# A gated SSD layer on one core: turnings in one step, TensorE's order tied to each chunk, time-step products in score banks, and fewer stores

## The chip, the cores and the metric

The kernel runs on one core of a Trainium2 chip. The metric is the device time of one launch in microseconds, as the median of several runs. The engines are TensorE (PE, with its weight loads shown as PEld), VectorE (DVE), ScalarE (ACT), GpSimd (POOL) and SyncE (SP), which issues most of the DMAs.

## The reference

A small diffusion backbone of two layers over 1024 latent and 256 context tokens, 1024 wide. Layer 0 is gated windowed attention. Layer 1 is a gated state-space mixer (SSD) that scans in both directions. Each layer is: norm, modulation, mixer, gated residual add. The part that the change touches is layer 1's front and chunk pass:

```python
z, xbc, dt_raw = jnp.split(h @ w_in, [SSD_WIDTH, SSD_WIDTH + SSD_CONV_DIM], axis=-1)
xbc = jax.nn.silu(centred_depthwise_conv(xbc, conv_w, conv_b))     # 5 taps
xs, bm, cm = jnp.split(xbc, ...)
dt = jax.nn.softplus(dt_raw... + dt_bias_dir)
...
a_cs = jnp.cumsum(da, axis=2)                                      # per chunk of 128
states = jnp.einsum('bcsgn,bcsgr,bcsgrp->bcgrpn', bm, decay_to_end, xdt)
h = exp(a_last) * h + states                                       # scan over chunks
cb = jnp.einsum('bcqgn,bcsgn->bcqsg', cm, bm)
y_diag = jnp.einsum('bcqsg,bcqsgr,bcsgrp->bcqgrp', cb, lmat, xdt)
y_off = jnp.einsum('bcqgn,bcgrpn,bcqgr->bcqgrp', cm, h_prev, jnp.exp(a_cs))
```

There are 8 groups of 4 heads of 64, a state of 128, 8 latent chunks of 128 tokens and 2 context chunks. All is float32.

## The kernel before, in words

Large products are split: each operand is a high part in a fast form and a low part, and three products (high by high, low by high, high by low) add up in one bank. `weights` makes the parts of a weight tile: ScalarE casts the high part (L1034), VectorE subtracts for the low part (L1038). There are two buffers of each.

Layer 1 goes through the groups. While group g's eight chunks run (`slot`, once a chunk), the projections of group g+1 (`front`) fill TensorE between a chunk's steps. `front` is a generator: each `next` issues one product and yields its cost, and `run` in the main loop takes as many as the chunk's share. Its products are:

- L1085, a context tile, 24 products of 256 columns into a bank called psD, of which there is one buffer,
- L1095, the two latent tiles of 512 columns, into pj (two buffers),
- L1129, the z gate, 192 products of 256 columns.

Each finished tile goes through side steps kept in the queue `post`, which lets one go after so much TensorE work: a first tap on ScalarE (L1007), four taps on VectorE (L1011), tanh on ScalarE (L1018), product on VectorE (L1019), and then `natural`: the tile is turned by TensorE (L1058) into the bank that its raw product came from, and ScalarE copies it out (L1061), into bn or xn.

A chunk (`slot`) consists of the opening products pcb (L1247) and po (L1249 from the forward state hf, L1250 from the backward state hb), the state product L1256, four head products L1281 against the masked decay tile M, and the turning of the chunk before (L1312, copied by ScalarE's L1313). M is made from rows loaded from DRAM: `load_rows` (L1221), an offset on POOL (L1226), a merge on VectorE (L1230), four exponentials on ScalarE (L1236), the product with pcb (L1251). VectorE also makes L1260, L1266, L1292 and L1293 of each chunk, and the z gate's product L1140.

`states` is the chain that carries the states from chunk to chunk: product L1198 into psD, decay on POOL, addition on VectorE (L1210) or a copy on ScalarE (L1202). Each L1198 needs the psD buffer back from the step ahead.

Ahead of group 0 stands the time step. `dt_raw` adds the bias on ScalarE (L923) to 3 products per slice of a narrow weight (`proj`, L246 to L248). The `dt_chain` steps (VectorE L974 to L987, among them the reciprocal L980) make softplus, decays and running sums, and store the sums and the totals to DRAM, from where the rows of M and the totals (eal) are loaded. `dt_tail` spaces these steps by DTPACE. Layer 0 ends with a norm whose sum is L363 and whose spread is L380.

The order of the instructions on each engine is set by a scheduler at build time from the program's order and the tiles' dependencies. `issue_after(x)` holds what is issued in its block behind instruction x. Each engine then executes its list in that order.

## Time and profile before

| | before |
|---|---|
| median of 3 runs | 1810.02 us (1809.37 to 1811.35) |
| profiled execution | 1807.02 us |
| its span | 1805.3 us |
| mean granted clock | 0.993 |
| first pcb (L1247) of groups 0, 1, 2, 3 at | 849.29, 954.77, 1060.54, 1166.32 us |

The profiled execution is 1.7 us longer than its span and 3.0 us below the median. The times of layer 1 lie between about 735 us and the end. The pcb starts show the length of a group, some 105.7 us, of which nearly all is TensorE work.

### The profile page before, as it was taken

The page shows a single profiled execution, that of the slowest core. Times are in us where ns is not written, and L with a number is a line of the kernel's source. Part 1 is how long each engine was busy: PE and PEld are TensorE (multiplying, and loading weights), DVE is VectorE, ACT ScalarE, POOL GpSimd, SP SyncE. Part 2 cuts the span into 40 slices and gives each one's busy share as a digit, 9 for nine tenths or more (in the row PEclk, how much of TensorE's full clock was granted, in tenths as well). Part 3 has the DMA queues.
Part 4 walks back from the last instruction along what each step waited for, and adds up shares of the span by engine and source line. Part 5 has one row for each costly group of instructions (what it writes and reads, how often), then busy time and mean ns, then how long its engine had stood idle before and what let it go on. Part 6 is the DMA issues. An engine that isn't in the chain of part 4 may idle for free.

```text
span 1805.3 us, 28983 instructions
## 1 busy us (share of the span) xinstructions
PE 1739.6 (96%) x10319; PEld 1494.7 (83%) x10319; DVE 1181.8 (65%) x2115; ACT 867.1 (48%) x1906; POOL 799.0 (44%) x1068
## 2 busy tenths in 40 slices
PE   6899999999999999999999999999999999999997
PEld 2697788888888887778888898988889898888887
DVE  4634436778877885684776858577684867766734
ACT  3612237777777774452443525344353534544522
POOL 2331127555575545103454544645454464554411
PEclk9999999999999999999999999999999999999999
DMA  9558856444455436222222323222332322656533
GB/s 334 226 144 268 283 177 149 106 100 111 111 153 130 120 102 221 73 53 73 71 77 82 92 62 98 79 71 79 81 93 62 100 73 76 174 169 170 175 101 121
DMA packets 212495, 227.61 MB, mean 126 GB/s; under 512 B 16384, under 2 KB 149632, under 8 KB 212352
## 3 DMA queue, kind: packets, MB, share of 16 engines
q1 hardware_dynamic: 178288, 207.12, 38.0%
q0 software_dynamic: 34064, 18.65, 5.8%
q8 instruction: 81, 1.33, 0.3%
q14 instruction: 62, 0.51, 0.1%
HBM read 190.88 MB, written 35.13 MB: 125 GB/s over the span
## 4 chain that ended last, share of the span: by engine, by line
PE 81%; DVE 9%; ACT 4%; DMA 3%; issue 2%; SPq 1%; POOL 1%; DVEq 0%; ACTq 0%; POOLq 0%
PE pj L1095 17%; PE pj L1129 10%; PE pj L1527 7%; PE pj L246 6%; PE pj L247 6%; PE pj L248 6%; PE psD L1085 4%; PE psX L1281 3%; PE pt L684 3%; PE psD L1198 2%; PE pv L691 2%; PE pv L690 1%; PE S L659 1%; PE S L658 1%; PE psX L1249 1%
## 5 line engine op out<-in xcount | busy, mean ns | idle before, releaser
L246 PE MATMUL pj<-uH,wh 128*128 128x512 f32 (+1 forms) x712 | 257.4, 363 | 9.0 <-ACT uH L470 6.3
L247 PE MATMUL pj<-uL,wh 128*128 128x512 f32 (+1 forms) x712 | 243.3, 342 | 0.5 <-POOL uL L707 0.4
L248 PE MATMUL pj<-uH,wl 128*128 128x512 f32 (+1 forms) x712 | 242.4, 341 | 1.4 <-POOL wl L231 1.4
L1095 PE MATMUL pj<-uH,wl 128*128 128x512 f32 x512 | 172.7, 405 | 0.0
L1095 PE MATMUL pj<-uH,wh 128*128 128x512 f32 x512 | 171.4, 405 | 1.2 <-ACT bn L1061 0.7
L1095 PE MATMUL pj<-uL,wh 128*128 128x512 f32 x512 | 169.2, 402 | 0.0
L246 PEld LDWEIGHTS pj<-uH,wh 128*128 128x128 f32 x712 | 135.6, 191 | 36.2 <-ACT uH L470 7.7
L1129 PE MATMUL pj<-wh,uH 128*128 128x256 f32 x512 | 150.3, 294 | 9.1 <-ACT xn L1061 9.1
L1173 POOL TENSOR_TENSOR xw<-xn,dtdec 128x256 f32<-128x256 f32 x144 | 92.9, 650 | 141.6 <-PE psD L1198 107.1
L1129 PE MATMUL pj<-wh,uL 128*128 128x256 f32 x512 | 152.7, 298 | 0.0
L248 PEld LDWEIGHTS pj<-uH,wl 128*128 128x128 f32 x712 | 135.0, 190 | 18.6 <-POOL wl L231 2.3
L247 PEld LDWEIGHTS pj<-uL,wh 128*128 128x128 f32 x712 | 135.8, 191 | 16.0 <-issue 3.0
L1129 PE MATMUL pj<-wl,uH 128*128 128x256 f32 x512 | 146.7, 287 | 0.0
L689 DVE TENSOR_TENSOR pl<-pt,ph 128x512 fp32r<-128x512 f32 x168 | 114.1, 688 | 47.2 <-ACT ph L688 46.2
L231 POOL TENSOR_TENSOR wl<-wr,wh 128x512 fp32r<-128x512 f32 x76 | 100.2, 1322 | 86.1 <-ACT wh L229 85.2
L663 DVE CUSTOM_DVE_ANT_0 sm<-S,mask,nsink 128x640 f32<-128x640 f32 (+2 forms) x160 | 119.2, 773 | 19.8 <-PE S L659 12.6
L665 ACT ACTIVATE sm<-sm,nm 128x640 f32<-128x640 f32 (+2 forms) x160 | 118.6, 742 | 16.6 <-DVE nm L663 15.9
L688 ACT CAST ph<-pt 128x512 fp32r<-128x512 f32 x168 | 97.5, 586 | 56.0 <-PE pt L684 52.7
L229 ACT CAST wh<-wr 128x512 fp32r<-128x512 f32 (+1 forms) x116 | 74.7, 648 | 87.7 <-PE pj L247 63.5
L1095 PEld LDWEIGHTS pj<-uH,wl 128*128 128x128 f32 x512 | 95.3, 188 | 19.2
L1095 PEld LDWEIGHTS pj<-uL,wh 128*128 128x128 f32 x512 | 95.4, 188 | 18.7
L1129 PEld LDWEIGHTS pj<-wh,uH 128*128 128x128 f32 x512 | 98.7, 193 | 13.5 <-ACT xn L1061 12.1
(339 smaller groups left out, 4810.8 us busy)
## 6 DMA issues: line engine op xcount, KB each, us to landing
wr<-w_x SPq DMA_DIRECT2D x32, 512.0 KB, 4.6
M<-acs SPq DMA_DIRECT2D x64, 256.0 KB, 4.9
bw<-acs SPq DMA_DIRECT2D x64, 256.0 KB, 5.5
wr<-w_sk SPq DMA_DIRECT2D x24, 512.0 KB, 3.8
wr<-wg SPq DMA_DIRECT2D x40, 256.0 KB, 4.5
qs<-q POOLq DMA_DIRECT2D x40, 256.0 KB, 3.9
wada<-w_ada SPq DMA_DIRECT2D x16, 512.0 KB, 7.2
wr<-wq SPq DMA_DIRECT2D x32, 256.0 KB, 3.0
```

The source lines that it names most:

```text
L231: (eng or nc.vector).tensor_tensor(l, raw, h, op=ALU.subtract)
L246: self.nc.tensor.matmul(ps, lh, rh, start=first and i == 0, stop=False)
L247: self.nc.tensor.matmul(ps, lh, rl, start=False, stop=False)
L248: self.last_mm = self.nc.tensor.matmul(ps, ll, rh, start=False, stop=last and i == n - 1)
L663: nc.vector.tensor_tensor_reduce(out=sm[:, :W], in0=Sv, in1=self.mask[:, m0 : m0 + W], scale=-SCALE, scalar=self.nsink[:, 4 * j + r : 4 * ...
L665: nc.scalar.activation(sm[:, :W], sm[:, :W], AF.Exp, bias=nm[:, r : r + 1], scale=-1.0, accum_out=sums[:, r : r + 1])
L688: nc.scalar.copy(ph, ptf)
L689: nc.vector.tensor_sub(pl, ptf, ph)
L1095: nc.tensor.matmul(raw[:, 512 * i : 512 * i + 512], l[:, k, :], r[i][:, k, :], start=k + y == 0, stop=k == KT - 1 and y == 2)
L1129: nc.tensor.matmul(pj[:, c], l, r[:, k, :], start=c % 2 + q + k + y == 0, stop=c % 2 == 1 and q == 1 and k == 3 and y == 2)
L1173: nc.gpsimd.tensor_tensor(xw, X(st, c).rearrange("p (r h) -> p r h", r=R), self.dtdec[:, c, hd(d, g)].unsqueeze(2).broadcast_to([P, R, HP] ...
L1527: nc.tensor.matmul(banks[x], l[:, z, sl], r, start=k == 2 * qs[0] and y == 0, stop=k == 2 * qs[-1] + 1 and y == 2)
```

## The change

It has five parts.

1. `natural` issues all the turnings of a tile in one step, and then the copies. Before, a tile with two destinations was turned by halves, with a copy behind each half.
2. TensorE's order is tied per chunk: every piece that `run` takes from `front` or `ssd_out` is held behind the latest L1250 (`self.opened`), and pcb is held behind the latest such product (`self.pe`).
3. The time-step products move from the start of layer 1 into the end of layer 0, in score banks (tag S): those of the context tile ahead of the last norm, and those of the first latent tile in two halves, one behind the norm's sum and one behind its spread (`dt_first`).
4. The time-step chain: 1/(1+e) and two operations become a tanh on ScalarE and two fused operations; the rows of M are asked for directly behind the running sums' store, not at the end; the stores become 4 (from 8) and 2 (from 12), with EPOS for the changed column order; DTPACE goes from 1.0 to 1.6.
5. The first merge is held behind the last silu product (`silu_last`).

```diff
-DTPACE = 1.0
+DTPACE = 1.6
+EPOS = (0, 1, 5, 6, 3, 4, 8, 9, 2, 7)
...
-                for f in steps:
+                for f in steps[:1] + ([self.dt_first] if i == 1 else []) + steps[1:]:
                     f()
...
             self.dt_setup()
-            for i, lo in ((2, 256), (0, 0)):
-                n = TT[i][1] // 2
-                self.dt_raw(self.dts[:, lo : lo + n], self.proj(ps, self.wdt, i), n)
+            raw = self.proj(ps, self.wdt, 2, "S")
+
+            def dt_first():
+                self.dt_raw(self.dts[:, 256:384], raw, 128)
+                out = []
+                half = self.proj_g(out, ps, [self.wdt], self.uH, self.uL, 0, "S", parts=2)
+                with self.tc.issue_after(self.summed.ins):
+                    next(half)
+                with self.tc.issue_after(self.spread.ins):
+                    next(half, None)
+                self.dt_raw(self.dts[:, :256], out[0], 256)
...
         def decay():
-            for o in (0, 384):
-                for y in range(4):
-                    d, s = y // 2, (o // 384) * 512 + 256 * (y % 2)
-                    nc.sync.dma_start(self.acs_d[32 * d : 32 * d + 32, s : s + 256], w3[32 * y : 32 * y + 32, o : o + 256])
+            for d in range(2):
+                for o in range(2):
+                    dst = self.acs_d[32 * d : 32 * d + 32, 512 * o : 512 * o + 512].rearrange("r (h n) -> h r n", h=2)
+                    nc.sync.dma_start(dst, w3[64 * d : 64 * d + 64, 384 * o : 384 * o + 256])
...
+            for d in range(2):
+                nc.sync.dma_start(self.eal_d[0, 32 * d : 32 * d + 32].rearrange("r (h k) -> h r k", h=2), et[64 * d : 64 * d + 64])
...
+            lambda: act(wr, w1, AF.Tanh, scale=-0.5),
             lambda: act(w1, w1, AF.Exp),
...
-            lambda: v.reciprocal(w3, w2),
-            lambda: v.tensor_mul(w1, w1, w3),
-            lambda: v.tensor_add(w1, w1, ea),
+            lambda: v.scalar_tensor_tensor(w1, in0=wr, scalar=1.0, in1=w1, op0=ALU.add, op1=ALU.mult),
+            lambda: v.scalar_tensor_tensor(w1, in0=w1, scalar=0.5, in1=ea, op0=ALU.mult, op1=ALU.add),
...
             decay,
+            rows,
             total,
...
             lambda: act(ea, w3, AF.Exp),
-            rows,
...
-            def tr(lo, hi):
-                for x in range(lo, hi):
+
+            def tr():
+                for x in range(n):
                     nc.tensor.transpose(raw[:, x * P : (x + 1) * P], acc[:, x * P : (x + 1) * P], self.ident)
...
-            for d, lo, hi in dst:
-                steps.append(lambda lo=lo, hi=hi: tr(lo, hi))
-                steps.append(lambda d=d, lo=lo, hi=hi: ev(d, lo, hi))
-            return [(LATE, steps)]
+            return [(LATE, [tr] + [lambda d=d, lo=lo, hi=hi: ev(d, lo, hi) for d, lo, hi in dst])]
...
-            nc.tensor.matmul(pcb, st["bT"][:, cs], st["cT"][:, cs], start=True, stop=True)
+            with self.tc.issue_after(self.pe.ins):
+                nc.tensor.matmul(pcb, st["bT"][:, cs], st["cT"][:, cs], start=True, stop=True)
...
-            nc.tensor.matmul(po[:, 256:], st["cT"][:, cs], flat(st["hb"][c]), start=True, stop=True)
+            self.opened = nc.tensor.matmul(po[:, 256:], st["cT"][:, cs], flat(st["hb"][c]), start=True, stop=True)
...
-        merge(fw[0], bw.pop(0))
+        with self.tc.issue_after(self.silu_last.ins):
+            merge(fw[0], bw.pop(0))
...
                     while spent < until:
-                        cost = next(work, None)
-                        if cost is None:
-                            return
-                        spent += cost
-                        post.run(cost)
+                        with self.tc.issue_after(self.opened.ins):
+                            cost = next(work, None)
+                            if cost is None:
+                                return
+                            spent += cost
+                            post.run(cost)
```

Three places show how the order moves. In the rows of the changed kernel the line numbers are its own: its L1068 is L1058 of before, L1071 is L1061, L1092 is L1085, L1102 is L1095, L1205 is L1198, L1255 is L1247, L1257 and L1258 are L1249 and L1250, L1264 is L1256, L1289 is L1281, L1320 is L1312, L1015 is L1007, L1045 is L1034, L1321 is L1313 and L1303 is L1295.

TensorE, end of chunk 2 in group 2, before. pj takes latent products, psD context products; ident is the matrix of a turning.

```order
5596 L1095 MATMUL pj_2684_11995<-uH_2132_8670,wl_11884 128x512
5597 L1058 MATMUL psD_11781<-ident_63,cctx_11829 128x128 x2
5598 L1312 MATMUL psX_11925<-ident_63,y_2155_8749 128x128
5599 L1249 MATMUL psX_12028<-hf_11899,cT_11245 128x256
5600 L1250 MATMUL psX_12028<-hb_2613_11573,cT_11245 128x256
5601 L1058 MATMUL pj_2659_11830<-ident_63,bT_11831 128x128 x4
5602 L1256 MATMUL psX_12032<-xw_11975,bn_2455_10692 128x256
5603 L1281 MATMUL psX_12057<-xn_2452_10689,M_11842 128x64 x4
5604 L1085 MATMUL psD_11957<-uH_1654_6747,wh_11882 128x256
```

The same place now:

```order
5615 L1102 MATMUL pj_2685_11982<-uH_2131_8637,wl_11871 128x512
5616 L1320 MATMUL psX_12049<-ident_63,y_2156_8751 128x128
5617 L1068 MATMUL pj_2660_11817<-ident_63,bT_11818 128x128 x8
5618 L1068 MATMUL psD_11944<-ident_63,cctx_11981 128x128 x2
5619 L1092 MATMUL psD_12109<-uH_1654_6747,wh_12065 128x256
```

Between a psD turning and the next context product four kinds of chunk products stood; now nothing stands there, and the eight turnings of bT are one block ahead of it.

ScalarE at that place, before (the copy of the psD tile is the fourth row):

```order
968 L1061 COPY bn_2647_11776<-pj_2659_11830 128x512
969 L1295 ACTIVATE y_2671_11903,ss_11948<-y_2156_8751 128x257
970 L1007 ACTIVATE cacc_11996<-pj_2684_11995,cb_8724,cw_8721 128x1024
971 L1061 COPY bn_2649_11778<-psD_11781 128x256
972 L1313 ACTIVATE uT_11926<-psX_11925,nw_8727 128x128
```

And now (the copy of the psD tile is the last row):

```order
975 L1045 CAST wh_12240<-wr_12107 128x1024
976 L1015 ACTIVATE cacc_11983<-pj_2685_11982,cb_8724,cw_8721 128x1024
977 L1321 ACTIVATE uT_12050<-psX_12049,nw_8727 128x128
978 L1071 COPY bn_2648_11763<-pj_2660_11817 128x512
979 L1071 COPY bn_2649_11764<-pj_2660_11817 128x512
980 L1071 COPY xn_2647_11762<-psD_11944 128x2x128
```

A weight cast, a first tap and three more rows are queued ahead of the psD copy.

TensorE, chunk 0 of group 0, before. The rows left out are L1095: 12, 22 and 13 products. L1198 is the chain's product.

```order
4396 L1247 MATMUL psX_9601<-cT_9227,bT_8798 128x128
4397 L1249 MATMUL psX_9603<-hf_2218_9297,cT_9227 128x256
4398 L1095 MATMUL pj_2275_9662<-uH_2034_8170,wh_9539 128x512
...
4411 L1198 MATMUL psD_9464<-xw_9441,bn_2161_8760 128x256
...
4434 L1198 MATMUL psD_9489<-xw_9462,bn_2161_8760 128x256
4435 L1256 MATMUL psX_9607<-xw_9487,bn_2161_8760 128x256
4436 L1281 MATMUL psX_9644<-xn_2158_8757,M_9099 128x64 x4
...
4450 L1250 MATMUL psX_9603<-hb_2251_9491,cT_9227 128x256
```

And now:

```order
4393 L1255 MATMUL psX_9588<-cT_9161,bT_8798 128x128
4394 L1257 MATMUL psX_9590<-hf_2217_9260,cT_9161 128x256
4395 L1205 MATMUL psD_9430<-xw_9407,bn_2161_8760 128x256
4396 L1205 MATMUL psD_9451<-xw_9428,bn_2161_8760 128x256
4397 L1205 MATMUL psD_9476<-xw_9449,bn_2161_8760 128x256
4398 L1264 MATMUL psX_9594<-xw_9474,bn_2161_8760 128x256
4399 L1289 MATMUL psX_9631<-xn_2158_8757,M_9087 128x64 x4
4400 L1258 MATMUL psX_9590<-hb_2252_9478,cT_9161 128x256
4401 L1092 MATMUL psD_9609<-uH_1654_6747,wh_9526 128x256
```

The chunk's products and three products of the chain now stand together, ahead of all projections of the chunk.

More of the change, by code (lines that the diff above doesn't have):

```diff
@@ L362, in rstd_c @@
         for b in range(n // P):
-            nc.tensor.matmul(pn[:, b : b + 1], acc[:, b * P : (b + 1) * P], self.ones[:, 0:1], start=True, stop=True)
+            self.summed = nc.tensor.matmul(pn[:, b : b + 1], acc[:, b * P : (b + 1) * P], self.ones[:, 0:1], start=True, stop=True)
         return self.rstd_n(pool, pn, n, width, size, rout, dout, scalar)
@@ L379, in rstd_n @@
         pr = t(ps, [P, 512], F32, self.ptag)
-        nc.tensor.matmul(pr[:, :n], self.ones, dg.rearrange("p b n -> p (b n)"), start=True, stop=True)
+        self.spread = nc.tensor.matmul(pr[:, :n], self.ones, dg.rearrange("p b n -> p (b n)"), start=True, stop=True)
         r = t(*(rout or (pool, [P, size], F32, f"rr{size}")))[:, :n]
@@ L848, in attention @@
             self.dt_setup()
-            for i, lo in ((2, 256), (0, 0)):
-                n = TT[i][1] // 2
-                self.dt_raw(self.dts[:, lo : lo + n], self.proj(ps, self.wdt, i), n)
+            raw = self.proj(ps, self.wdt, 2, "S")
[8 more added lines that the diff above has]
+                self.dt_raw(self.dts[:, :256], out[0], 256)
+            self.dt_first = dt_first
             for _ in steps[-1]():
@@ L931, in dt_chain @@
         w1, w2, w3, ea = [t(p, [P, KT // 2, 256], F32, y).rearrange("p a b -> p (a b)")[:, :n] for y in ("xn4", "sz", "sz", "xn4")]
+        wr = t(p, [P, LAT], F32, "bT")[:, :n]
         tot = t(self.pc, [P, 8], F32, "tot", 2)[:, :nb]
@@ L946, in total @@
             act(et, tot, AF.Exp)
-            for y in range(4):
-                d, h = y // 2, y % 2
-                row = self.eal_d[0][32 * d : 32 * d + 32]
-                for o, c in ((0, 2 * h), (3, 4 + 2 * h)):
-                    nc.sync.dma_start(row[:, c : c + 2], et[32 * y : 32 * y + 32, o : o + 2])
-                nc.sync.dma_start(row[:, 8 + h : 9 + h], et[32 * y : 32 * y + 32, 2:3])
+            for d in range(2):
+                nc.sync.dma_start(self.eal_d[0, 32 * d : 32 * d + 32].rearrange("r (h k) -> h r k", h=2), et[64 * d : 64 * d + 64])
             nc.sync.dma_start(self.eal, self.eal_d.broadcast_to([P, 64, NCH + NCC]))
@@ L1017, in silu, with prod @@
         nc = self.nc
-        return [lambda: nc.scalar.activation(raw, acc, AF.Tanh),
-                lambda: nc.vector.scalar_tensor_tensor(acc, in0=raw, scalar=1.0, in1=acc, op0=ALU.add, op1=ALU.mult)]
+        def prod():
+            self.silu_last = nc.vector.scalar_tensor_tensor(acc, in0=raw, scalar=1.0, in1=acc, op0=ALU.add, op1=ALU.mult)
+        return [lambda: nc.scalar.activation(raw, acc, AF.Tanh), prod]
     def front(self, g, st, post, first=None, dt=None):
@@ L1053, in natural @@
         def natural(raw, acc, dst, o, n):
-            steps = []
-            def tr(lo, hi):
-                for x in range(lo, hi):
+            def tr():
+                for x in range(n):
                     nc.tensor.transpose(raw[:, x * P : (x + 1) * P], acc[:, x * P : (x + 1) * P], self.ident)
@@ L1084, in front @@
                     for y, (l, r) in enumerate(((wh, uH), (wh, uL), (wl, uH))):
-                        nc.tensor.matmul(raw, l[:, k, :], r[2][:, k, :], start=k + y == 0, stop=k == KT - 1 and y == 2)
+                        self.pe = nc.tensor.matmul(raw, l[:, k, :], r[2][:, k, :], start=k + y == 0, stop=k == KT - 1 and y == 2)
                         yield N256
@@ L1094, in front @@
                         for i in q:
-                            nc.tensor.matmul(raw[:, 512 * i : 512 * i + 512], l[:, k, :], r[i][:, k, :], start=k + y == 0, stop=k == KT - 1 and y == 2)
+                            self.pe = nc.tensor.matmul(raw[:, 512 * i : 512 * i + 512], l[:, k, :], r[i][:, k, :], start=k + y == 0, stop=k == KT - 1 and y == 2)
                             yield N512
@@ L1127, in front @@
                         for y, (l, r) in enumerate(((u, ww["h"]), (u, ww["l"]), (v, ww["h"]))):
-                            nc.tensor.matmul(pj[:, c], l, r[:, k, :], start=c % 2 + q + k + y == 0, stop=c % 2 == 1 and q == 1 and k == 3 and y == 2)
+                            self.pe = nc.tensor.matmul(pj[:, c], l, r[:, k, :], start=c % 2 + q + k + y == 0, stop=c % 2 == 1 and q == 1 and k == 3 and y == 2)
                             yield N256
@@ L1177, in decay @@
         def decay(hn, h, g, c, d):
-            nc.gpsimd.tensor_tensor(hn, h, self.eal[:, hd(d, g), c].unsqueeze(2).broadcast_to([P, R, HP]), op=ALU.mult)
+            nc.gpsimd.tensor_tensor(hn, h, self.eal[:, hd(d, g), EPOS[c]].unsqueeze(2).broadcast_to([P, R, HP]), op=ALU.mult)
         def flat(x):
@@ L1526, in ssd_out @@
                         for y, (l, r) in enumerate(((w["h"], hi), (w["h"], lo), (w["l"], hi))):
-                            nc.tensor.matmul(banks[x], l[:, z, sl], r, start=k == 2 * qs[0] and y == 0, stop=k == 2 * qs[-1] + 1 and y == 2)
+                            self.pe = nc.tensor.matmul(banks[x], l[:, z, sl], r, start=k == 2 * qs[0] and y == 0, stop=k == 2 * qs[-1] + 1 and y == 2)
                             yield N512
```

## The prediction

> **What bounds the kernel now.** The page's busy times come first.

> ```profile
> PE 1739.6 (96%) x10319; PEld 1494.7 (83%) x10319; DVE 1181.8 (65%) x2115; ACT 867.1 (48%) x1906; POOL 799.0 (44%) x1068
> ```

> TensorE (PE) works for 96% of the span, and its products are the same before and after. So the change can move only the rest, in which PE stands still. The windows say where that is (length, then busy time of PE, PEld, DVE, ACT, POOL, then the granted clock).

> ```profile
> 734.00:780.00 46.00, 43.41 (x228) 36.66 (x227) 31.07 (x43) 23.49 (x37) 1.02 (x1) 1.00 0.23 77
> 780.00:820.00 40.00, 33.37 (x171) 26.39 (x169) 31.37 (x43) 22.31 (x55) 2.78 (x4) 0.98 0.31 62
> 1030.00:1136.00 106.00, 104.47 (x650) 93.62 (x650) 72.95 (x124) 45.29 (x107) 53.30 (x76) 1.00 0.30 81
> ```

> The order before 734 us is unchanged. From 734 to 820 us, the transition from the attention layer into the SSD's first group, PE idles for 2.6 + 6.6 = 9.2 us. In 106 us of steady groups it idles 1.5 us. PE's waits give the causes (us in total, times, longest): first those of the transition alone, then the one row that a steady group has.

> ```profile
> PE pj L1058 <- DVE cacc L1019: 2.9, 2, 2.3
> PE pj L246 <- ACT cacc L923: 1.5, 1, 1.5
> PE psD L1085 <- ACT cacc L923: 1.1, 1, 1.1
> PE pj L1058 <- ACT bn L1061: 1.1, 1, 1.1
> PE pj L1095 <- ACT bn L1061: 0.7, 1, 0.7
> PE pj L1058 <- ACT xn L1061: 0.6, 1, 0.6
> PE pj L1095 <- ACT xn L1061: 0.5, 1, 0.5
> PE pj L1058 <- DVE bT L1019: 0.5, 1, 0.5
> ```

> ```profile
> PE pj L1129 <- ACT xn L1061: 9.1, 7, 1.3
> ```

> So two budgets stand against each other: about 9 us once, and 1.3 us in each of seven groups, where the z projection L1129 waits until ScalarE has copied the last turned block.

> **The transition.** VectorE's timeline and the chain of waits show its largest hole (the last two VectorE rows serve further down):

> ```profile
> 815.05 0.73 DVE L1230 COPY_PREDICATED M<-before,bw 128x512 f32<-128x512 int32 x1 [5.26 <-POOL bw L1226]
> ...
> 815.92 1.22 DVE L1019 SCALAR_TENSOR_TENSOR cacc<-pj,cacc 128x1024 f32<-128x1024 f32 x1
> ...
> 849.08 0.42 DVE L1210 TENSOR_TENSOR hb<-hb,psD 128x256 f32<-128x256 f32 x1 [3.24 <-PE psD L1198]
> ...
> 851.82 1.22 DVE L1038 TENSOR_TENSOR wl<-wr,wh 128x1024 fp32r<-128x1024 f32 x1
> ```

> ```profile
> 817.30 1.04 ACT wh L1034
> 818.35 1.10 ACT cT L1007
> 819.45 0.48 ACT xn L1061
> 819.93 0.04 issue
> 819.98 1.12 PE pj L1058 x4
> 821.09 0.85 PE psD L1198 x2
> 821.95 5.08 PE pj L1129 x30
> 827.03 0.43 PE psD L1198 x2
> 827.46 3.83 PE pj L1129 x32
> ```

> The first merge L1230 kept VectorE standing for 5.26 us while its row tiles were loaded. The silu product L1019 was queued behind it, and PE's turnings (L1058) behind that: 2.3 us, then 0.6. Then PE ran slowly: 30 z products took 5.08 us where 32 take 3.83 next, so 1.5 us were lost; a chain product took 0.85 us instead of 0.43, twice, and the two sets of four turnings about 0.5 us each too much. I put the clock's loss at 3.3 us. After the change the merge is ordered behind the last silu product, and the row tiles are asked for right after the scans, ahead of the totals' stores. VectorE is free and this hole goes. Late next is ScalarE: both copies of the turned block come behind a weight cast and a tap, 1.05 + 1.10 + 2 x 0.48 = 3.1 us by the chain, of which PE covers 0.86 with the eight turnings: a wait of 2.25 us.

> The time-step products in score banks wait no more for the bias step L923 (1.5 + 1.1 us). But the norm's spread product L380 now stands between their halves and waits for a diagonal that VectorE makes behind two low parts L1038 (1.22 us each): 2.0 us I estimate. The first projection starts 0.9 us earlier. The first bT turning takes all eight blocks at once and needs the whole of bT's silu. The reciprocal is gone from VectorE, but the tanh adds a step on ScalarE, and taps and time-step chain still alternate: I estimate 3.5 us (0.5 before), then 1.35 for the copies (1.8 before). The waits of 0.6 and 0.5 us later on go, and one chain product moves out behind the first chunk.

> Before, the last wait began at 814.9 us (817.2 less 2.3). Now PE is there at 814.9 - 0.9 + 3.0 - 0.45 - 1.1 = 815.4, its turnings included in what 2.25 leaves over, and goes on at about 817.5. Then stand 192 z products of 0.12 us (3.83/32) and eight chain products of 0.43, 26.5 us: the first chunk starts at 844.0 instead of 849.3 us (the pcb product ahead of the L1249 row below), **-5.4 us** with rounding. Bounds: -12.5 with all waits and the clock's loss gone, 0 with none. Fewer stores, the sparser chain steps and two table loads fewer lie on queues that only this sum hangs on; the sparser steps are covered by projections, and where that fails it is in the 3.5 us.

> **Group 0, chunk 0.** PE's timeline:

> ```profile
> 849.51 0.60 PE L1249 MATMUL psX<-hf,cT 128*128 128x256 f32 x2
> ```

> Before, 13 and 22 projections stood between this chunk's chain products L1198, and PE did not wait. Now projections may come only behind L1250, which stands last, so three L1198 are consecutive. Each needs VectorE's L1210 (0.42 us) of the one ahead. The first ends at 849.51 + 0.43 + 0.43 = 850.4; its L1210 is queued behind the z product L1140, which has run to 851.8 and takes a tanh of its own first, so PE goes on at 852.3: 1.9 us. The third waits behind L1038: 1.2 us. **+3.1** (bounds 0, with VectorE ahead, and 4.3, with one L1038 more). In group 7 L1250 waits for a state in the same way: **+0.65** (0 to 1.2).

> **The steady groups.** The tie puts this at the end of chunk 2 in groups 0 to 6: fifteen L1095, a turning of y (L1312), eight turnings of bT, two of a context tile in psD, and at once the context projection L1085, which needs the one psD buffer again. It waits until ScalarE has copied the turned tile out. Before, other products lay between; PE's and ScalarE's timelines in group 2:

> ```profile
> 1092.05 0.38 PE L1058 MATMUL psD<-ident,cctx 128*128 128x128 f32 x2
> 1092.26 0.27 PE L1312 MATMUL psX<-ident,y 128*128 128x128 f32 x1
> ...
> 1095.17 0.36 PE L1085 MATMUL psD<-uH,wh 128*128 128x256 f32 x1
> ```

> ```profile
> 1093.83 0.36 ACT L1061 COPY bn<-psD 128x256 f32<-128x256 f32 x1
> 1094.08 0.38 ACT L1313 ACTIVATE uT<-psX,nw 128x128 f32<-128x128 f32 x1
> 1094.34 0.52 ACT L1300 ACTIVATE y<-y,ss 128x256 f32<-128x256 f32 x1
> ```

> The copy came out at 1094.2, 1.9 us behind the turning, hidden because PE asked for psD only at 1095.17. Now, with the end of the psD turnings' steps as zero: the ten turnings and L1312 take 1.2 us at 0.107 each (1092.05 to 1092.26 for two), so the tap's bank was complete at -1.2, and the cast, whose buffer is read until two products earlier, is released at -1.65. A product ends 0.17 us behind its step (0.38 busy against 0.21). In ScalarE's order stand cast 1.05, tap 1.10, L1313 0.26, two copies of 0.48 and the psD copy 0.36: -1.65 + 0.17 + 3.73 = 2.25, and 0.05 to PE. **+2.3 us in seven groups, +16.1.** Bounds: 0 if ScalarE has cast and tapped by then; 2.8 if a scaling L1300 (0.52) comes ahead too.

> The old stall before L1129 shrinks: the eight turnings run first and then both copies, which PE partly covers with chain products. I take 0.75 (bounds 0 and 1.3): **-0.55 seven times, -3.9**. The pcb product, tied behind the last projection, reads tiles long finished and costs nothing itself; but behind a projection that waits, the opening products wait too, and with them VectorE's M product.

> Does each new hole also cost the clock?

> ```profile
> 80.00:82.00 2.00, 0.51 (x4) 0.51 (x5) 2.00 (x6) 0.16 (x1) 0.48 (x1) 1.00 0.00 0
> 816.00:818.00 2.00, 0.66 (x4) 0.42 (x4) 1.14 (x2) 2.00 (x6) 0.52 (x1) 1.00 0.59 119
> 818.00:820.00 2.00, 1.25 (x3) 0.53 (x3) 1.62 (x2) 2.00 (x4) 1.22 (x3) 0.54 0.56 146
> ```

> From 814.9 to 818 PE worked 0.66 us and the clock fell to 0.54; with 1.5 us idle at 80 to 82 it stayed at 1.00. A hole of 2.3 us with full work on both sides lies between; I take the clock as kept. [...]

> **Sum.** -5.4 + 3.1 + 0.65 + 16.1 - 3.9 = +10.6 us. The profiled execution took 1807.0 us (1805.3 of span), 3.0 below the median 1810.0. It becomes 1817.6, and the median 1820.6.

> **Rivals.** (a) *Faster:* ScalarE is ahead at the end of chunk 2, so that the psD copy follows its turning at once. With that term at zero the sum is -5.5 us: 1804.5; with group 0's first chunk hidden also, 1801.4. It decides at a stall of 0.8 us a group ((5.4 + 3.9 - 3.75)/7). For it: ScalarE is busy only 48%. Against: the order ahead of the copy, and that cast and tap both need products which PE ends within the last 1.7 us. 24%.

> (b) *The clock falls* behind each new hole, 3.3 us as in the transition: 7 x 3.3 = 23 more, 1844. For it 818 to 820, against it 80 to 82 us. 5%.

> (c) *The transition does not give*: the row tiles come early, but bT's wait and the last copies eat the gain. Without the 5.4: 1826. 10%.

> (d) *Nothing in sum*: the new stall is near 0.8 us, 1810. 7%.

> **How the numbers follow.** Within 0.2%, 3.6 us, a measurement of this kernel can hardly tell a difference. The forecast has 54%. Slower is 54 + 5 + 10 = 69%, the same 7%, faster 24%. The forecast's own range is 1814 to 1828: 0.5 us a group either way is 3.5, the transition and group 0 some 3 to 4 more. To hold 8 in 10 it reaches down to most of (a) and takes in (c): 1803 to 1829.

> **What would show it.** Right: among PE's waits a row of L1085 on ScalarE's L1061, seven times and 2 to 2.5 us each; the L1129 row at 4 to 6 us; groups some 1.8 us longer than before; the first pcb near 844 us; L1198 waiting for L1210 behind it, 3 us. Wrong: no such L1085 row, groups no longer than before, or a clock under 0.9 in them.

## The result: slower by 1.4%, more than forecast

| | before | after |
|---|---|---|
| median | 1809.69 us (4 runs, 1806.54 to 1811.35) | 1834.41 us (4 runs, 1833.71 to 1836.07) |
| ratio | | 1.0136, 95% interval 1.0119 to 1.0153 |
| profiled execution, span | 1807.02, 1805.3 us | 1833.99, 1832.3 us |

The change costs 24.7 us; the forecast was +10.6, its range ended at 1829. In the changed kernel's rows the line numbers are its own, as listed with the order above (L1136 is L1129, L1068 is L1058, L1071 is L1061). First its waits of PE in the transition, then the rows that matter of the whole execution:

```profile
PE pj L1068 <- DVE bT L1028: 3.2, 1, 3.2
PE pt L381 <- DVE dg L379: 2.1, 1, 2.1
PE pj L1136 <- ACT xn L1071: 1.7, 1, 1.7
PE pj L1102 <- ACT bn L1071: 1.2, 1, 1.2
PE pj L1102 <- ACT xn L1071: 0.3, 1, 0.3
```

```profile
PE psD L1092 <- ACT xn L1071: 18.1, 7, 2.6
...
PE pj L1136 <- ACT xn L1071: 6.5, 8, 1.7
...
PE psD L1205 <- DVE hb L1217: 3.1, 2, 1.6
```

The waits that the prediction worked out are there, nearly at their size: bT 3.2 (forecast 3.5), the diagonal 2.1 (2.0), the last copies 1.7 (2.25), the new psD stall 2.6 seven times (2.3), the chain products 3.1 (3.1), the z stall 0.7 a group (0.75). Only L1250's wait in group 7 (0.65) has no row. ScalarE's and PE's timelines show the psD stall as it was walked through:

```profile
1105.59 1.03 ACT L1045 CAST wh<-wr 128x1024 fp32r<-128x1024 f32 x1
1106.53 1.20 ACT L1015 ACTIVATE cacc<-pj,cb,cw 128x1024 f32<-128x1024 f32 x1
1107.63 0.35 ACT L1321 ACTIVATE uT<-psX,nw 128x128 f32<-128x128 f32 x1
1107.88 1.05 ACT L1071 COPY bn<-pj 128x512 f32<-128x512 f32 x2
1108.82 0.38 ACT L1071 COPY xn<-psD 128x256 f32<-128x256 f32 x1
```

```profile
1106.30 0.38 PE L1068 MATMUL psD<-ident,cctx 128*128 128x128 f32 x2
1109.26 0.39 PE L1092 MATMUL psD<-uH,wh 128*128 128x256 f32 x1 [2.58 <-ACT xn L1071]
```

But the waits do not add up to the time. A stage by stage ledger from the two traces, in us. The first mark is the spread product (L380 before, L381 now) of the norm ahead of the last one, the others are the first pcb of each group:

| stage | before | after | difference | forecast |
|---|---|---|---|---|
| to that spread product, late in layer 0 (same order in both) | 696.94 | 695.00 | -1.9 | 0 |
| from there to the first pcb | 152.35 | 149.72 | -2.6 | -5.4 |
| group 0 | 105.48 | 115.69 | +10.2 | +4.9 |
| groups 1 to 5, each | 105.78 | 109.3 | +3.5 | +1.8 |
| group 6 | 105.35 | 108.86 | +3.5 | +1.8 |
| group 7 and the end | 216.29 | 216.54 | +0.3 | +0.7 |

The first line is scatter and not the change: up to that mark TensorE's order is the same in all kernels of this document, and in their eleven traces it is reached between 694.8 and 702.9 us. From the mark to the end the change costs 28.9 us in these two traces.

A steady group loses 2.0 us by waits (2.6 + 0.7 - 1.3) and 1.5 to 1.7 us by something else. The windows of two stalls, with the granted clock behind the five busy times, say what:

```profile
996.99:1000.40 3.41, 0.82 (x8) 0.59 (x6) 2.95 (x3) 3.38 (x7) 0.08 (x1) 1.00 0.64 102
1000.40:1003.81 3.41, 3.41 (x15) 2.96 (x13) 3.37 (x6) 0.00 (x0) 0.00 (x0) 0.51 0.43 149
1106.22:1109.63 3.41, 0.83 (x8) 0.59 (x6) 2.94 (x3) 3.40 (x7) 0.09 (x1) 1.00 0.40 73
1109.63:1113.04 3.41, 3.41 (x15) 2.96 (x13) 3.38 (x6) 0.00 (x0) 0.00 (x0) 0.51 0.48 167
```

Behind the hole TensorE is granted half the clock (0.51 in these rows) for 3.4 us, which costs 1.7 us, half of it, in each of groups 1 to 6. The same stands in the transition (two slow windows behind the bT stall, the first three rows) and in group 0 (two behind the chain products, the next three):

```profile
778.58:781.99 3.41, 0.20 (x1) 0.00 (x0) 3.35 (x5) 3.41 (x4) 0.00 (x0) 1.00 0.07 20
781.99:785.40 3.41, 2.23 (x9) 1.83 (x10) 3.35 (x6) 1.90 (x6) 0.00 (x0) 0.50 0.31 88
785.40:788.82 3.42, 3.42 (x9) 2.68 (x10) 3.38 (x5) 0.33 (x1) 0.00 (x0) 0.50 0.30 92
846.80:850.22 3.42, 1.14 (x4) 0.59 (x4) 2.42 (x5) 0.07 (x1) 2.62 (x3) 1.00 0.16 25
850.22:853.63 3.41, 3.41 (x14) 2.90 (x13) 0.84 (x2) 0.00 (x0) 2.54 (x5) 0.51 0.35 129
853.63:857.04 3.41, 3.41 (x17) 3.32 (x15) 1.09 (x2) 0.00 (x0) 1.90 (x3) 0.50 0.34 62
887.76:891.18 3.42, 2.01 (x15) 1.60 (x13) 1.43 (x2) 3.42 (x9) 0.55 (x1) 1.00 0.47 106
891.18:894.59 3.41, 2.24 (x15) 2.11 (x15) 3.34 (x3) 1.53 (x4) 0.00 (x0) 1.00 0.77 196
```

The last two rows are group 0's own psD stall, of the same 2.6 us, and there the clock was kept. The place of the hole differs. From group 0 to group 6 the slow phases of this trace begin at 850.3, 1000.4, 1109.7, 1218.9, 1328.1, 1437.3 and 1546.6 us: 44, 32, 32, 32, 32 and 32 times 3.413 us apart. Cut into windows of that length from these starts, the trace has the whole hole in one window at 996.99 and 1106.22 (0.8 us busy), and in group 0 across two (2.0 and 2.2). And a group of 109.3 us is 32.0 windows, so the hole falls in the same place each time. That the work left in one such window decides the clock was my estimate from these rows; the runs put it to the test.

### The profile page after: what moved, and what is told of

It reads as the page before. It is cut to its first block, busy times and chain, and to the rows that moved or that the text cites. A ratio compares the mean times of both kernels' runs of the same rounds, so it can differ in the third digit from the quotient of the medians.

```text
span 1832.3 us, 28943 instructions
## 1 busy us (share of the span) xinstructions
PE 1749.4 (95%) x10319; PEld 1505.3 (82%) x10319; DVE 1178.2 (64%) x2114; ACT 867.9 (47%) x1905; POOL 794.8 (43%) x1068
## 4 chain that ended last, share of the span: by engine, by line
PE 53%; ACT 3%; DVE 2%; POOL 1%; issue 1%; DMA 0%; DVEq 0%; ACTq 0%; POOLq 0%
PE pj L1102 17%; PE pj L1136 10%; PE pj L1537 7%; PE psD L1092 4%; PE psX L1289 3%; PE psX L1258 2%; PE psD L1205 2%; PE psX L1257 2%; PE psX L1264 1%; PE pj L249 1%; PE psX L1255 1%; PE pj L247 1%; PE pj L248 1%; PE psX L1320 1%; ACT M L1243 1%
## 5 line engine op out<-in xcount | busy, mean ns | idle before, releaser
L1102 PE MATMUL pj<-uH,wh 128*128 128x512 f32 x512 | 170.1, 404 | 1.4 <-ACT bn L1071 1.2
L1102 PE MATMUL pj<-uH,wl 128*128 128x512 f32 x512 | 170.4, 406 | 0.0
L1102 PE MATMUL pj<-uL,wh 128*128 128x512 f32 x512 | 166.8, 399 | 0.0
L247 PEld LDWEIGHTS pj<-uH,wh 128*128 128x128 f32 x712 | 135.6, 191 | 34.5 <-issue 6.3
L1136 PE MATMUL pj<-wh,uH 128*128 128x256 f32 x512 | 149.2, 291 | 6.5 <-ACT xn L1071 6.5
L1136 PE MATMUL pj<-wh,uL 128*128 128x256 f32 x512 | 153.1, 299 | 0.0
L1136 PE MATMUL pj<-wl,uH 128*128 128x256 f32 x512 | 150.8, 295 | 0.0
L249 PEld LDWEIGHTS pj<-uH,wl 128*128 128x128 f32 x712 | 134.9, 190 | 18.1 <-POOL wl L232 1.8
L248 PEld LDWEIGHTS pj<-uL,wh 128*128 128x128 f32 x712 | 135.7, 191 | 16.1 <-DVE uL L472 3.2
L1102 PEld LDWEIGHTS pj<-uL,wh 128*128 128x128 f32 x512 | 96.5, 189 | 20.1
L1102 PEld LDWEIGHTS pj<-uH,wl 128*128 128x128 f32 x512 | 96.5, 189 | 19.1
L1102 PEld LDWEIGHTS pj<-uH,wh 128*128 128x128 f32 x512 | 94.1, 189 | 19.9 <-ACT bn L1071 1.6
```

Source lines behind the costliest of these rows:

```text
L247: self.nc.tensor.matmul(ps, lh, rh, start=first and i == 0, stop=False)
L248: self.nc.tensor.matmul(ps, lh, rl, start=False, stop=False)
L249: self.last_mm = self.nc.tensor.matmul(ps, ll, rh, start=False, stop=last and i == n - 1)
L1102: self.pe = nc.tensor.matmul(raw[:, 512 * i : 512 * i + 512], l[:, k, :], r[i][:, k, :], start=k + y == 0, stop=k == KT - 1 and y == 2)
L1136: self.pe = nc.tensor.matmul(pj[:, c], l, r[:, k, :], start=c % 2 + q + k + y == 0, stop=c % 2 == 1 and q == 1 and k == 3 and y == 2)
```

## The experiments

The theory T: the tie leaves nothing between a psD turning and the next context product; the hole of 2.6 us and the half clock behind it are the steady loss, and the same pair is in group 0's first chunk. The rival R: turning in one step makes the hole. For the clock there were two theories more, H (any such hole halves it) and W (the hole's place on the grid of these windows does). All ratios are against runs of the kernel before on the same chip; the times themselves come from several chips, so small differences between two variants are read from the traces, from the mark in layer 0 on.

**1. The tie taken out** (part 2 undone).

```diff
-            with self.tc.issue_after(self.pe.ins):
-                nc.tensor.matmul(pcb, ...)
+            nc.tensor.matmul(pcb, ...)
...
-                        with self.tc.issue_after(self.opened.ins):
-                            cost = next(work, None)
+                        cost = next(work, None)
```

> The changed kernel with part 2 undone: neither the projections nor pcb are held behind a chunk's products. Theory T (the tie empties the space between a psD turning and the next context product, a hole of 2.6 us in each of seven groups, and the clock halves behind it for one window of 3.4 us; in group 0's first chunk two more holes and two slow windows): the psD row is gone from PE's waits, no granted clock under 1.00 in groups 1 to 6, groups of about 105.7 us; 1834 - 7 x 3.5 - 6.7 = about 1803 (1799 to 1808). Rival R (the turnings in one step, with both copies behind them, make the hole whatever the tie): the psD row stays at some 18 us, 1825 or more.

Measured: 1824.21 us (1819.43 to 1829.02), ratio 1.0091 (1.0065 to 1.0116). The psD row is gone, so R fell, and groups 0 to 3 took 103.7 to 104.3 us, with PE never idle in group 1 (a window of the length of that group):

```profile
948.30:1052.20 103.90, 103.90 (x653) 93.66 (x652) 72.50 (x123) 45.72 (x105) 54.13 (x74) 1.00 0.30 81
```

But 1803 was missed. Without the tie each group's order differs from the last: the latent products issued in chunk 0 grow from 62 in group 0 to 94 in group 4. From group 4 on waits come back; from 1260 to 1620 us the chain products alone wait about 9 us. What T had left out is that the tie gives this kernel the same order in every group. The kernel before has that without a tie: 48 latent products in chunk 0 of group 0 and 50 in those of groups 1 to 6.

**2. The tie alone**, part 2 on the kernel before.

> The kernel before with part 2 alone added. T: the psD holes and slow windows are there without the turnings in one step, about 0.5 us shorter each since only one of the two wide copies is ahead of the psD copy; no gain of the transition; 1832 to 1842. R: near 1810, no psD row.

Measured: 1860.43 us (1858.95 to 1860.85), ratio 1.029 (1.0273 to 1.0307). R's time fell again, but T's row did not come either: no L1085 waits for L1061, and the loss is nearly twice what T said. PE's waits:

```profile
PE pj L1058 <- ACT bn L1061: 13.9, 8, 2.3
PE pj L1058 <- ACT xn L1061: 9.3, 8, 2.2
PE psD L1198 <- ACT hx L1202: 8.2, 3, 2.7
```

A turning in two halves has its second half wait for the copy of the first. Before, chunk products stood between the halves; under the tie nothing does. Behind a psD turning PE stands at the same place as in the changed kernel, but for that second half, and the psD copy is out before L1085 asks:

```profile
1117.80 0.38 PE L1058 MATMUL psD<-ident,cctx 128*128 128x128 f32 x2
1119.93 0.66 PE L1058 MATMUL pj<-ident,bT 128*128 128x128 f32 x4 [1.75 <-ACT bn L1061]
1120.60 0.38 PE L1085 MATMUL psD<-uH,wh 128*128 128x256 f32 x1
```

So the tie as written loses with either form of the turnings; the psD row itself appears only where the tie and the turnings in one step (part 1) meet. Under the tie, part 1 takes these waits of the halves away. How much it saves is not measured alone: of the 26.9 us between this run's span and the changed kernel's, 7.4 lie ahead of the first pcb, where parts 3 to 5 and the scatter of layer 0 act, and 21.8 in groups 0 to 6.

**3. Work put into the hole.** Twelve extra turnings into the unused half of the psD bank, behind the psD turning.

```diff
                     nc.tensor.transpose(raw[:, x * P : (x + 1) * P], ...)
+                if fillup is not None:
+                    for x in range(12):
+                        nc.tensor.transpose(fillup, acc[:, :P], self.ident)
```

> The changed kernel with twelve extra turnings (1.28 us, results unused) written into the free half of the psD bank behind the psD turning that precedes the hole, in groups 1 to 7's fronts. T with the clock as the second cause: the wait falls from 2.6 to about 1.3 us since the extra work lies inside it, PE is then busy for over half of any 3.4 us, the clock stays at 1.00, and six or seven slow windows of 1.7 us are saved: about 1823 (1821 to 1825), faster in spite of more work. Rival H (the clock halves behind any such hole, or the slow rows are not the cause of the time): 1834 or more; if the copy waits for the extra turnings as well, 1834 + 9 = 1843.

Measured: 1828.74 us (1827.90 to 1831.44), ratio 1.0114 (1.0095 to 1.0134), a miss of the 1821 to 1825 that T gave. It is 5.7 us less than the changed kernel, in spite of 9 us of useless work, but from another chip, and the intervals of the two ratios overlap. The traces are clearer: from the mark in layer 0 to the end this one takes 7.8 us less, no window of groups 1 to 6 is slow, and their length is 108.0 us (107.6 the last) instead of 109.3. The saving is smaller than 11 us since the copy now comes 0.4 us later: the rest of the wait is 1.7 us, not 1.3. The window of the hole and the one behind it, in this run:

```profile
1111.34:1114.75 3.41, 1.72 (x16) 1.48 (x14) 3.37 (x3) 2.62 (x6) 0.00 (x0) 1.00 0.52 100
1114.75:1118.16 3.41, 3.41 (x27) 3.25 (x26) 3.38 (x6) 0.00 (x0) 1.23 (x2) 1.00 0.33 119
```

In the window behind the hole 27 products run where the changed kernel has 15: the half clock is a cause of time, and with 1.7 us of work in the hole's window it did not come. That holds for groups 2 and 5, where the whole hole lay in one window. A group of 108.0 us is 31.6 windows, so in the other four the hole lay across two, and there its place may have kept the clock, as in run 4.

**4 and 5. Work put far from the hole**, sixteen or thirty-two turnings in chunk 5 of groups 0 to 6, into a free part of pcb's bank.

```diff
+            if c == 5 and g < G - 1:
+                for x in range(16):
+                    nc.tensor.transpose(pcbank[:, 256 : 256 + P], st["bT"][:, cs], self.ident)
```

> The changed kernel with sixteen extra turnings (1.7 us, unused) in chunk 5 of groups 0 to 6, far from the hole, which stays as long as it is. Theory W (the clock is decided on a grid of fixed windows of 3.41 us that runs free of the program; the groups of 109.3 us are 32.0 windows, so once the hole falls inside one window it does so in every group): a halved group becomes 111.0 us = 32.5 windows, the next hole lies across two windows, nothing is halved, the group is 109.3 = 32.0 windows and stays unhalved; so at most one or two slow windows in groups 1 to 6, and 12 us of extra work cost only 1 to 5 us: 1835 to 1839. Rival H (the hole by itself halves the clock): slow windows in all of groups 1 to 6, 1834 + 12 = 1846.

> As pad16 with twice as many extra turnings, 3.4 us in chunk 5 of groups 0 to 6, which is one whole window of the grid. Theory W (grid of 3.41 us windows free of the program): a halved group becomes 109.3 + 3.4 = 112.7 us = 33.0 windows, so the hole falls into the same place of a window again and every group from the first halved one on is halved, as in the changed kernel itself; six or seven slow windows; 1834 + 24 = 1858 (1854 to 1862). Rival E (with pad16 the clock was kept because there is more work in the group or because its order differs elsewhere): no slow windows here either, groups of 110.8 us, 1846 to 1850.

Measured with 16: 1845.18 us (1842.61 to 1847.99), ratio 1.0207 (1.0186 to 1.0228). The time lies nearer to H, and the groups decide for W: they took 109.07 us, less than without the extra 1.7 us, the psD row is unchanged (18.1 us, seven times), and no window of groups 1 to 6 is slow. The time beyond W's came elsewhere: group 7 and the end took 224.4 us instead of 216.5, where PE waited 1.4 and 4.1 us for the turnings of L1324 with two slow windows about the second wait (its cause stays open), and the first pcb came 4.1 us later than in the changed kernel, 1.7 of them lost already by the mark in layer 0, up to which the order is the same. With 32: 1855.22 us (1850.15 to 1858.99), ratio 1.0231 (1.0214 to 1.0249), and slow windows are back in four of groups 1 to 6, which E said could not be. W said six or seven. The hole's window and the next, twice in the run with 16 extra turnings, then twice with 32:

```profile
1217.42:1220.84 3.42, 2.23 (x16) 1.78 (x14) 1.21 (x2) 3.42 (x8) 0.55 (x1) 1.00 0.45 106
1220.84:1224.25 3.41, 2.01 (x13) 1.91 (x14) 3.27 (x5) 1.75 (x5) 0.00 (x0) 1.00 0.67 193
1326.65:1330.06 3.41, 2.07 (x15) 1.64 (x13) 1.35 (x2) 3.41 (x9) 0.55 (x1) 1.00 0.42 103
1330.06:1333.48 3.42, 2.17 (x15) 2.04 (x15) 3.28 (x6) 1.60 (x4) 0.00 (x0) 1.00 0.75 184
```

```profile
1009.30:1012.71 3.41, 0.83 (x7) 0.59 (x6) 3.08 (x3) 3.27 (x7) 0.00 (x0) 1.00 0.53 88
1012.71:1016.13 3.42, 3.42 (x13) 2.97 (x12) 3.38 (x6) 0.00 (x0) 0.00 (x0) 0.50 0.45 153
...
1234.58:1237.99 3.41, 1.77 (x12) 1.69 (x13) 3.34 (x4) 2.00 (x6) 0.00 (x0) 1.00 0.76 172
1237.99:1241.41 3.42, 3.42 (x28) 3.26 (x26) 3.42 (x8) 0.65 (x1) 1.08 (x2) 1.00 0.15 46
```

With 16 the hole lies across two windows in group after group. With 32 a halved group took 112.0 us, 32.8 windows and not the 33.0 expected, so the hole wanders, and in groups 3 and 6 it got by with 1.8 us of work in its window (the last two rows are group 3, which took 110.6 us).

**6. The hole taken away, the tie kept.** The psD turning is asked for earlier, and the products behind it are held behind it.

```diff
+                    last = nc.tensor.transpose(raw[:, x * P : (x + 1) * P], acc[:, x * P : (x + 1) * P], self.ident)
+                if late != LATE:
+                    self.turned = last
...
+                post.extend(... + natural(raw, acc, ..., nat[1], 2, 8.0 if n == 1 and g > 0 else LATE))
...
-                        with self.tc.issue_after(self.opened.ins):
+                        with self.tc.issue_after(self.opened.ins), self.tc.issue_after((self.turned or self.opened).ins):
```

> The changed kernel with one place reordered, the tie kept: the psD turning that preceded the hole is asked for some 2.8 us of products before the end of chunk 2, and the products behind it are held behind it on TensorE. So twelve latent products stand between the turning and the next context product, and ScalarE's copies come ahead of the cast and the tap. T (hole and slow window are the steady loss): the psD row falls below 3 us in all, no granted clock under 1.00 in groups 1 to 6, groups of some 105.5 us instead of 109.3; 1834.4 - 7 x 3.7 = about 1808 (1805 to 1813). Rival S (the tie costs in itself, the wait only moves to another product): another row of 10 us or more, 1820 or more.

Measured: 1810.50 us (1805.33 to 1815.12, 10 runs), ratio 1.0003 (0.9990 to 1.0015). The psD row is gone, no window of groups 1 to 6 is slow, and the groups took 105.1 us, less than before (105.8). S fell: one place in the order is the whole steady loss.

**7. Chunk 0 of group 0 not tied.**

```diff
-                        with self.tc.issue_after(self.opened.ins):
+                        with self.tc.issue_after(self.opened.ins) if g or spent > total / NCH else nullcontext():
```

> The changed kernel with the projections of chunk 0 of group 0 alone not held behind L1250, so that 27 of them stand between the first and the second chain product again. T: the two waits of 1.6 and 1.5 us of the chain products go, and with them the two slow windows behind them (3.4 us of loss); the steady groups are as before; 1834.4 - 6.5 = about 1828 (1826 to 1830). If only the waits count: 1831.

Measured: 1833.28 us (1832.08 to 1837.06), ratio 1.0128 (1.0114 to 1.0142), a miss of 5 us. The chain products' row is gone, and group 0 took 111.45 us instead of 115.69. But a slow window moved to 931 us in it, and the same bT stall in the transition was followed by 10.2 us of slow clock here instead of 6.8, after an earlier slow window at 747 us, so that the first pcb came 153.0 us behind the mark in layer 0 instead of 149.7. Group 1 had no slow window here (107.55 us), groups 2 to 6 had theirs. From the mark on this trace takes 3.0 us less than the changed kernel's.

**8. Both 6 and 7.**

> Both edits together, the reordered turning and chunk 0 of group 0 not tied. T: the two gains add, since they lie in different places: about 1802 (1798 to 1806), faster than the kernel before by the transition's 4.6 us and a little less waiting in the groups. Rival S: 1813 or more.

Measured: 1804.79 us (1799.85 to 1805.55, 5 runs), ratio 0.9961 (0.9948 to 0.9975): faster than both kernels, if by 0.4% only. The time lies in the range that T gave, but the gain does not lie where T put it: of 4.8 us against the trace before, the transition gave 1.2 (T said 4.6), and groups 1 to 6 gave 3.6 with 105.1 us each for 105.8. A steady group has one stall left, 0.8 us, and the full clock:

```profile
1069.20:1174.30 105.10, 104.26 (x652) 93.72 (x651) 73.05 (x123) 45.30 (x107) 54.51 (x74) 1.00 0.33 81
```

**9. Parts 3, 4 and 5 alone**, with the halved turnings and no tie.

> The kernel before with parts 3, 4 and 5 alone (time-step products, chain, stores, first merge), without the turnings in one step and without the tie. T for the transition: the first pcb comes 4 to 5 us earlier than before. For the rest the scheduler's order without the tie decides, and it is not the order of before (projections and chunk products are bunched): if that costs nothing 1805; if the order drifts as without the tie alone, 1815 to 1830.

Measured: 1816.98 us (1815.49 to 1819.92), ratio 1.0037 (1.0023 to 1.0050). The order hardly drifts (29 latent products in chunk 0 of each group 0 to 6), but it is not that of before: a group takes some 107.0 us, and seven waits of L1268 on POOL, 6.5 us, are new. What these parts bring is thus not separated from what the order does: the time to the first pcb, from the mark in layer 0, was 151.6 us, against 152.4 before.

## Why the prediction was right in sign and wrong in size

- *The psD stall:* right, in place and cause; 2.6 us for 2.3. Runs 1 and 6 show that the order there is what makes it.
- *The z stall, group 0's chain products, the transition's waits:* right within 0.6 us each, but for group 7's, which has no row. The first pcb came at 844.7 us, as forecast (844), by luck: layer 0 was 1.9 us early, and the transition gave 2.6 us and not 5.4.
- *"A hole of 2.3 us with full work on both sides lies between; I take the clock as kept":* this is the step that failed. The terms of the sum that it left out: 1.7 us in six groups (10 us), two slow windows in group 0 (3.4 us) and two behind the bT stall (3.4 us, which is why the transition gave 2.6 and not 5.4). Together 17 us; with the 10.6 of the sum that is 27.6, against 28.9 from the mark in layer 0 on (27.0 between the whole spans). Rival (b) had the clock's loss at 3.3 us a hole, from the transition before, where two windows (818.16 to 824.99 us) were at 0.50; one window, as behind the new hole, is 1.7. The prediction gave it 5%.
- *Why the step failed:* it compared lengths of holes (1.5 us idle of 2 kept the clock, 2.3 and more lost it) and asked which was nearer. Length alone did not decide here: the same stall of 2.6 us kept the clock in group 0, with 2.01 and 2.24 us of work in its two windows, and lost it in group 1, with 0.82 in one. On the grid of the trace before, the two holes that the prediction compared differ in place too: that of 80 to 82 us lies across two windows with 1.68 and 2.81 us of work, that at 815 us leaves 0.80 in one.

```profile
77.47:80.89 3.42, 1.68 (x12) 1.24 (x10) 3.42 (x7) 0.88 (x2) 0.18 (x1) 1.00 0.00 0
80.89:84.30 3.41, 2.81 (x23) 2.81 (x24) 3.41 (x6) 1.54 (x4) 1.44 (x1) 1.00 0.00 0
814.75:818.16 3.41, 0.80 (x6) 0.43 (x5) 2.09 (x4) 2.29 (x6) 0.94 (x3) 1.00 0.58 105
818.16:821.58 3.42, 2.81 (x8) 1.73 (x8) 3.17 (x3) 2.49 (x5) 1.89 (x3) 0.50 0.73 207
```

- *Group 0:* 3.1 of waits, 3.4 of clock, 2.0 by psD and z stalls and 0.4 for the moved chain product make 8.9 of the 10.2 us; the rest was not placed.

## What to carry to other kernels

When an order is tied, list what now stands between a buffer's release and its next use on the engine that needs it, and walk the releasing engine's own queue to that point: here it gave all waits but one within 0.6 us. Then price each hole twice, once as idle time and once as the clock behind it: in the changed kernel a hole that left TensorE 0.20 to 1.17 us of work in one window of 3.41 us was followed by one or two windows at half clock, 1.7 or 3.4 us more by half of each. There the groups of 109.3 us, 32.0 windows, repeated the loss six times. Twelve unneeded products in the hole (run 3), or a turning moved by 3 us (run 6), took it away.

## What the runs showed of the hardware

| PE busy in the window | windows | followed by half clock |
|---|---|---|
| 0.20 to 1.17 us | 11 | 11 |
| 1.68 to 1.87 us | 9 | none |
| 1.97 to 2.61 us | 17 | none |
| 2.62 us and more | 982 | none |

In the other runs the two sides overlap. The window of run 2 below, with 1.64 us of work, was followed by half clock, and so were windows with 1.91 us in run 4 (852.09 to 855.50 us) and in run 5 (858.95 to 862.36 us); those with 1.72 us in run 3 and 1.77 in run 5, shown there, were not. So busy time alone, as the profile counts it, gives no sharp limit in these traces; in the first 27 us of the program even a window with 2.30 us (22.86 to 26.27 us, before) and one with 2.10 us (20.82 to 24.23 us, changed kernel) were followed by half clock.

```profile
1117.52:1120.93 3.41, 1.64 (x13) 1.17 (x11) 2.82 (x3) 3.33 (x7) 0.00 (x0) 1.00 0.88 125
1120.93:1124.34 3.41, 3.41 (x13) 2.96 (x12) 2.77 (x5) 0.28 (x1) 0.00 (x0) 0.50 0.49 178
```

In the same two traces and the same stretch, full clock came back behind a first slow window with 3.02, 3.20 or 3.41 us of PE work, and not behind those with 2.23 (781.99 us, changed kernel) and 2.81 (818.16 us, before), so that the slow phase lasted two windows there. In run 4 one lasted three, with 1.97, 2.47 and 3.41 us of work in the windows from 783.82 us on. The full window at 850.25 us of the changed kernel, with 3.41 us, was followed by half clock once more, and its like in run 3 (855.00 us, 3.33) too. The changed kernel's groups are 32.0 windows (109.3 us) with the slow window in them; less the 1.7 us that it costs they would be 31.5.
